# A mixer layer on one core: conditioning weights in 2 MB pieces summed partly on TensorE, and block 0's stores issued from ScalarE's queue

## The chip, the cores and the metric

The kernel runs on one core of a Trainium2 chip. It uses TensorE (PE) for matrix products, VectorE (DVE), ScalarE (ACT) and GpSimd (POOL) for the element work, and SyncE (SP) mostly for issuing DMA transfers. The metric is device time in microseconds (us) of one execution; the median of 3 runs is what counts. Lower is better.

## The reference, cut to what matters

One layer (DEPTH is 1) on a sequence of 2048 tokens with 1024 features, in float32. The conditioning vector `c` gives shift, scale and gate (adaLN); the normalised input goes through one combined input projection into three groups of heads; their outputs are gated, concatenated, projected and added back:

```
mod = silu(c) @ w_ada + b_ada        # 1024 x 3072: shift, scale, gate
h   = rmsnorm(x, norm_g) * (1 + scale) + shift
u   = h @ w_in + b_in                # columns: mLSTM v,q,k,o,z; i,f gates; FoX; conv
A: mLSTM, 4 heads x 128 (q and k after a 4-tap convolution), chunk by chunk
B: forgetting attention, 4 heads x 64
C: 256 channels: a * sigmoid(g), 31-tap causal depthwise convolution, norm, silu
x   = x + gate * (concat(A, B, C) * silu(z) @ w_out);   out = rmsnorm(x, final_g)
```

## The kernel before, in words

The tokens are cut into 4 blocks of 512 (`TB`), the 1024 features into 8 tiles of 128 (`KT`). A product of float32 numbers is made from three products of float32r parts: every operand is split into a high part (a cast on ACT) and a low part (a subtraction), and hi·hi, hi·lo and lo·hi are summed on PE.

**The start of block 0.** `hprep(0, ada_k)` loads the four x tiles, normalises them, and then makes for each feature tile k the transposed input `hh0_k` (high) and `hl0_k` (low): four PE transposes `xT`, an ACT activation `hf = xT*gs + shift` (L148), an ACT cast `hh` (L151), a subtraction `hl` (L152). The two columns `gs` and `shift` of tile k come from `ada_k(k)`: the 1024 x 128 pieces of `w_ada` for shift and scale are loaded (tile `wa`, L747, two transfers of 512 KB for each k), multiplied by silu(c) and summed over 8 row groups: two of them start the sums on ACT (`wacc`, L772), six are added on DVE (L775), the two sums are added (L777), transposed on PE (`pt_ada`, L780), reduced on DVE (L782) and finished by three column operations (L784, L785, L787).

**The units of a block.** The input projection is cut into units of 256 columns or so. Their order is fixed: v (with the mLSTM gate columns), ca and cg (convolution group, value and gate), mv, mo, two qk units, mz, then mv to mz again for the other two heads, and the FoX and conv-gate units. A unit is 48 PE products of 512 columns, or 96 of 256. In block 0, `split_unit` gets the weights: for each half it loads 0.5 MB of raw weights into `wr` (L174, two buffers), casts the high part on ACT (L181) and subtracts the low part on POOL (L182), giving a 1 MB tile `w2`, three of which exist; it then stores that tile to DRAM as `wd` (L183), and blocks 1 to 3 load it from there instead of splitting again. Weights of a unit are fetched one unit or more ahead by `prefetch()`.

**After the v unit**, `gates()` runs scans on DVE (L350, L356, L363) and exponentials on ACT, and stores three small tables (`nb`, `rr`, `ir`, L352, L373, L374). **The convolution** of a block follows cg: for each of two channel tiles 31 taps; in block 0, 6 of these are products on ACT (`tp`, L458) added up on POOL (`ap`, L459), and the other taps are DVE operations (`ac`, L461, 24 and a first one on ACT). The qk units have a convolution of 4 taps on DVE (`am`, L552 and L556). The tiles `am` are transposed on PE (`pk`, L591) and multiplied with each other (`psT`, L595) in the mLSTM steps.

**What sets the order.** The program is written in stages, and the framework's scheduler decides in which order each engine gets its instructions; each engine then runs its own list in order. So an instruction that waits holds up everything behind it on its engine. On PE, `psT` and `pk` of the first two heads stand between the last product of the first mz unit and the first product of the second mv unit (`mv0_1`); this is so before and after the change. Before the change, all transfers that matter here are issued from SP: loads of raw weights, stores of split weights, and the loads of x for block 1 (`x1`, L129), whose normalisation (L135 to L138) is done as soon as the tiles have landed.

Of the kernel before, what the change touches and what calls it, by code (L numbers as in the profile page):

```python
# [16 lines left out]
P = 128  # L17
# [21 lines left out]
def tile_hybrid_trunk(  # L39
# [21 lines left out]
    v, s, g, pe, dma = nc.vector, nc.scalar, nc.gpsimd, nc.tensor, nc.sync  # L61
# [49 lines left out]
    wraw = left1.enter_context(tc.tile_pool(name="wraw", bufs=WRB))  # L111
# [11 lines left out]
    def hprep(b, pre=None):  # L123
# [34 lines left out]
    w_d = {}  # L158
# [5 lines left out]
    def split_unit(name, pieces, pool):  # L164
# [5 lines left out]
        for hf in range(2):  # L170
            wr = pool.tile([P, 4, 268], F32, name=f"wr_{name}_{hf}", tag="wr", bufs=WRA if pool is not wraw else 2)
            o = 0
            for col, n in pieces:
                dma.dma_start(  # L174
                    wr[:, :, o : o + n],
                    dram(w_in, hf * 4 * P * DIN + col, [[DIN, P], [P * DIN, 4], [1, n]]),
                )
                o += n
            flat, w4 = unit_tile(name, hf, width)
            wh, wl = w4[:, 0], w4[:, 1]  # L180
            s.copy(wh, wr[:, :, 0:width])  # L181
            (v if name in WLV else g).tensor_tensor(wl, wr[:, :, 0:width], wh.bitcast(F32), op=ALU.subtract)  # L182
            dma.dma_start(w_d[key][hf], flat.bitcast(F32))  # L183
            whs.append(wh)
            wls.append(wl)
# [127 lines left out]
    def unit_v(b, h):  # L313
        w = load_unit(f"v{b}")
        for tt in range(NTT):
# [13 lines left out]
            dma.dma_start(v_d[b * NTT + tt], vs.bitcast(F32))  # L329

    def gates(b, G):
# [20 lines left out]
        dma.dma_start(nb_d[:, b * TB : (b + 1) * TB], nbr)  # L352
# [20 lines left out]
        dma.dma_start(rr_d[b], rr)  # L373
        dma.dma_start(ir_d[b], ir)  # L374
# [284 lines left out]
    def wout_steps():  # L659
# [3 lines left out]
        def flat(name):  # L663
            return wraw.tile([P, 4, 268], F32, name=name, tag="wr", bufs=2).rearrange("p a e -> p (a e)")[:, 0:D]
# [49 lines left out]
    with tc.tile_pool(name="ada", bufs=4, side="right") as apool:  # L714
# [44 lines left out]
        def ada_k(j):  # L759
            if j < 0:  # L760
                for i in range(PRE):
                    ada_load(i)
                return
            if j == 0:
                for i in range(PRE, WAB):
                    ada_load(i)
            elif j + WAB - 1 < KT:
                ada_load(j + WAB - 1)
            wt = wts[j]
            accs = [apool.tile([P, 2, P], F32, name=f"wacc{j}{e}", tag=f"wacc{e}", bufs=2) for e in range(2)]  # L770
            for k in range(2):
                s.activation(accs[k], wt[:, k], AF.Identity, scale=csil[:, k : k + 1])  # L772
            for k in range(2, KT):
                a = accs[k % 2]
                v.scalar_tensor_tensor(a, wt[:, k], csil[:, k : k + 1], a, op0=ALU.mult, op1=ALU.add)  # L775
            acc = accs[0]
            v.tensor_tensor(acc, acc, accs[1], op=ALU.add)  # L777
# [415 lines left out]
WRB = 2  # L1193
# [45 lines left out]
```

## Time and profile before

| | us |
|---|---|
| median of 3 runs | 1372.14 (1370.55 to 1374.48) |
| the profiled execution | 1372.62 |
| its span in the profile | 1370.8 |
| PE busy | 1278.7 (93%) |
| DVE busy | 961.0 (70%) |
| ACT busy | 570.3 (42%) |
| POOL busy | 345.1 (25%) |
| mean DMA rate over the span | 220 GB/s |

The profile was taken of one execution, 0.5 us over the median; 1.8 us of its time lie outside its span. The page cuts the span in 40 slices of 34.3 us. PE is busy in 3, 7, 4 and 7 tenths of the first four slices, and in 9 or more in nearly all others. Stretches of time are given in us from the start of the span. In the rows that follow a line such as `L461` is the line of the kernel before, and `a<-b,c` says that tile a is written from tiles b and c.

### The profile page before, as it was taken

To read this page: it belongs to the slowest core of one execution; us is meant where nothing else is said; L and a number is where in the kernel's file an instruction comes from. 1 tells how busy PE (TensorE), PEld (TensorE's weight loads), DVE (VectorE), ACT (ScalarE), POOL (GpSimd) and SP (SyncE) were. 2 spreads that over 40 slices of the span, in tenths; PEclk is the share of its full clock that TensorE was granted. 3 is DMA by queue.
4 is the path that set the end of the run, shared out by engine and by line. 5 is a ranking of instruction groups with operands and counts; after the bars stand their busy time and mean duration, and the time that the engine had idled before them with its cause. 6 is when DMAs were issued, how large, how long until landed. Compare 5 with 4: busy or idle time off the path is not lost. (4 is left out here: it accounts for less than half of the span.)

```text
span 1370.8 us, 21119 instructions
## 1 busy us (share of the span) xinstructions
PE 1278.7 (93%) x7383; PEld 1112.9 (81%) x7383; DVE 961.0 (70%) x2473; ACT 570.3 (42%) x1204; POOL 345.1 (25%) x398
## 2 busy tenths in 40 slices
PE   3747999999999999999999999998989999999997
PEld 2637898887889888989888889988868888878886
DVE  6789948748997655794662796674786677866742
ACT  4472434354233236330314232224575565655631
POOL 3466545510132010050110070121131211211121
PEclk9977999999999999999999999999999999999999
DMA  9947768699897469564558764469986454644141
GB/s 266 321 170 235 239 231 292 230 320 397 305 347 246 155 221 314 186 214 167 188 189 270 217 242 173 168 228 326 294 263 183 152 173 143 198 149 134 62 131 62
DMA packets 151874, 301.62 MB, mean 220 GB/s; under 512 B 14968, under 2 KB 92072, under 8 KB 133592
## 3 DMA queue, kind: packets, MB, share of 16 engines
q1 hardware_dynamic: 151768, 300.28, 65.4%
q8 instruction: 58, 0.95, 0.3%
q14 instruction: 48, 0.39, 0.1%
HBM read 224.54 MB, written 75.69 MB: 219 GB/s over the span
## 5 line engine op out<-in xcount | busy, mean ns | idle before, releaser
L461 DVE SCALAR_TENSOR_TENSOR ac<-ca,dww,ac 128x512 f32<-128x512 f32 x228 | 181.5, 831 | 2.4 <-ACT ac L446 1.9
L1063 PE MATMUL po<-wo,yh 128*128 128x512 f32 x512 | 164.7, 397 | 1.0 <-ACT yh L1053 0.7
L287 PE MATMUL pc_qk<-hh,w_qk 128*128 128x512 f32 x512 | 163.1, 395 | 0.3 <-DMA w_qk<-wd_qk 0.3
L299 PE MATMUL pt_mv<-w_mv,hh 128*128 128x256 f32 (+1 forms) x512 | 100.4, 297 | 29.2 <-ACT w_mv L181 10.5
L879 ACT ACTIVATE S<-S,mx 128x512 f32<-128x512 f32 (+3 forms) x160 | 103.7, 651 | 52.4 <-DVE mx L877 48.8
L287 PEld LDWEIGHTS pc_qk<-hh,w_qk 128*128 128x128 f32 x512 | 96.2, 188 | 21.0 <-DMA w_qk<-wd_qk 0.6
L1063 PEld LDWEIGHTS po<-wo,yh 128*128 128x128 f32 x512 | 94.1, 188 | 21.0 <-ACT yh L1053 0.9
L299 PEld LDWEIGHTS pt_mv<-w_mv,hh 128*128 128x128 f32 x512 | 84.7, 202 | 31.1 <-ACT w_mv L181 10.9
L927 DVE TENSOR_TENSOR tl<-ptr,th 128x512 fp32r<-128x512 f32 (+1 forms) x144 | 92.4, 654 | 24.7 <-ACT th L926 23.7
L1063 PE MATMUL po<-wo,ya 128*128 128x512 f32 x256 | 101.1, 396 | 0.0
L299 PE MATMUL pt_mo<-w_mo,hh 128*128 128x256 f32 x512 | 96.9, 290 | 4.3 <-DMA w_mo<-wd_mo 2.2
L287 PE MATMUL pc_qk<-hl,w_qk 128*128 128x512 f32 x256 | 100.8, 394 | 0.0
L926 ACT CAST th<-ptr 128x512 fp32r<-128x512 f32 (+1 forms) x144 | 76.3, 561 | 51.2 <-PE ptr L918 50.3
L552 DVE SCALAR_TENSOR_TENSOR am<-um,cols,am 128x512 f32<-128x512 f32 x96 | 83.4, 877 | 10.1 <-ACT am L549 9.3
L918 PE MATMUL ptr<-ident,S 128*128 128x128 f32 x544 | 84.1, 275 | 4.8 <-DVE tl L927 3.4
L299 PEld LDWEIGHTS pt_mo<-w_mo,hh 128*128 128x128 f32 x512 | 82.0, 196 | 4.8 <-DMA w_mo<-wd_mo 2.4
L287 PE MATMUL pc_f<-hh,w_f 128*128 128x512 f32 x256 | 84.8, 400 | 0.0
L869 POOL TENSOR_SCALAR_AFFINE_SELECT nd<-n 128x128 f32<-128x128 f32 (+1 forms) x64 | 30.5, 479 | 208.4 <-DVE mx L872 129.0
L287 PE MATMUL pc_mz<-hh,w_mz 128*128 128x512 f32 x256 | 82.7, 395 | 0.0
L299 PE MATMUL pt_mv<-w_mv,hl 128*128 128x256 f32 (+1 forms) x256 | 74.7, 293 | 0.0
L299 PE MATMUL pt_mo<-w_mo,hl 128*128 128x256 f32 x256 | 73.4, 289 | 0.0
L918 PEld LDWEIGHTS ptr<-ident,S 128*128 128x128 f32 x544 | 64.5, 142 | 10.1 <-DVE tl L927 2.8
(267 smaller groups left out, 3245.0 us busy)
## 6 DMA issues: line engine op xcount, KB each, us to landing
w_qk<-wd_qk SPq DMA_DIRECT2D x24, 1024.0 KB
w_mo<-wd_mo SPq DMA_DIRECT2D x12, 1024.0 KB
w_mz<-wd_mz SPq DMA_DIRECT2D x12, 1024.0 KB
w_f<-wd_f SPq DMA_DIRECT2D x12, 1024.0 KB
w_mv<-wd_mv SPq DMA_DIRECT2D x10, 1024.0 KB
n<-nb_d SPq DMA_DIRECT2D x36, 256.0 KB
wa<-in_w_ada_dram SPq DMA_DIRECT2D x16, 512.0 KB
x<-in_x_dram SPq DMA_DIRECT2D x16, 512.0 KB
```

Of the source, the lines that this page charges most:

```text
L287: pe.matmul(ps, a, r, start=(n == 0), stop=(n == 3 * KT - 1))
L299: pe.matmul(ps[:, 0:width], a[:, cs], r, start=(n == 0), stop=(n == 3 * KT - 1))
L461: backlog.append(lambda acc=acc, u=u, i=2 * j + m, j=j: v.scalar_tensor_tensor(acc, u[:, j : j + TB], dww[:, i : i + 1], acc, op0=ALU.mult ...
L552: v.scalar_tensor_tensor(acc, u[:, j : j + TB], cols[:, r + 8 * j : r + 8 * j + 1], acc, op0=ALU.mult, op1=ALU.add)
L869: g.affine_select(out=nb[:, 0:Wq], in_=L["n", ch][:, 0:Wq], pattern=[[-1, Wq]], compare_op=ALU.is_ge, fill=NEG, base=t0 - ch * TB, channel ...
L879: s.activation(Sb[:, 0:Wq], Sb[:, 0:Wq], AF.Exp, bias=mx[:, 4:5], accum_out=mx[:, 8 + ch : 9 + ch])
L918: pe.transpose(pt[:, i, qi * P : (qi + 1) * P], Ps[qi][0][kk // TB][:, kk % TB : kk % TB + P], ident)
L926: s.copy(f(th), f(pt))
L927: v.tensor_tensor(f(tl), f(pt), f(th.bitcast(F32)), op=ALU.subtract)
L1063: pe.matmul(po, a, w[:, ns], start=(i == 0), stop=(i == 3 * KT - 1))
```

## The change

**The conditioning weights.** `w_ada` is loaded in four pieces of 2 MB instead of eight of 1 MB: one piece holds 256 columns of shift and 256 of scale, so the contiguous run in DRAM is 1 KB and not 512 bytes. A piece serves two feature tiles at once. Of its 8 row groups, one starts the sum on ACT (128x512), four are added by DVE operations of 128x512, and the last three are summed by PE, in products whose moving operand is one column of silu(c); a product of the DVE sum with a column of ones adds the rest. These are 16 products for a piece, straight in the layout of `shift` and `gs`, so the transpose and the reduction are gone. Three DVE operations on two columns finish the pair.

**The queues in block 0.** `sdma` is ACT's queue. From it are issued the stores of split weights, of v (L329) and of the three gate tables, the rows of small constants, the 8 and 4 column pieces of the v unit, and three of the later loads. The other loads stay on SP, so that the raw weight loads of block 0 follow one another there. The loads of `x1` are put behind the raw weights of `mz0_1` in the order of issue.

**The order of prefetches.** `ca0` gets its raw tiles from another pool and is fetched between the third and the fourth piece of `w_ada`; v between the first and the second.

```diff
-    v, s, g, pe, dma = nc.vector, nc.scalar, nc.gpsimd, nc.tensor, nc.sync
+    v, s, g, pe, dma, sdma = nc.vector, nc.scalar, nc.gpsimd, nc.tensor, nc.sync, nc.scalar
...
-            dma.dma_start(xt, x[0, b * TB + tt * P : b * TB + (tt + 1) * P, :])
+            with tc.issue_after(wload["mz0_1"]) if b == 1 else ExitStack():
+                dma.dma_start(xt, x[0, b * TB + tt * P : b * TB + (tt + 1) * P, :])
...
-                dma.dma_start(
-                    wr[:, :, o : o + n],
+                ins = (dma if n > 8 else sdma).dma_start(
+                    raw[:, :, o : o + n],
...
+                if n > 8:
+                    wload[name] = ins.ins
...
-            s.copy(wh, wr[:, :, 0:width])
-            (v if name in WLV else g).tensor_tensor(wl, wr[:, :, 0:width], wh.bitcast(F32), op=ALU.subtract)
-            dma.dma_start(w_d[key][hf], flat.bitcast(F32))
+            s.copy(wh, raw)
+            g.tensor_tensor(wl, raw, wh.bitcast(F32), op=ALU.subtract)
+            sdma.dma_start(w_d[key][hf], flat.bitcast(F32))
...
-            dma.dma_start(v_d[b * NTT + tt], vs.bitcast(F32))
+            (dma if b else sdma).dma_start(v_d[b * NTT + tt], vs.bitcast(F32))
...
-        dma.dma_start(nb_d[:, b * TB : (b + 1) * TB], nbr)
+        gdma = dma if b else sdma
+        gdma.dma_start(nb_d[:, b * TB : (b + 1) * TB], nbr)
...
-        dma.dma_start(rr_d[b], rr)
-        dma.dma_start(ir_d[b], ir)
+        gdma.dma_start(rr_d[b], rr)
+        gdma.dma_start(ir_d[b], ir)
...
-        def ada_load(j):
-            wt = apool.tile([P, KT, 2, P], F32, name=f"wa{j}", tag="wa", bufs=WAB)
+        def ada_load(jp):
+            wt = apool.tile([P, KT, 2, 256], F32, name=f"wa{jp}", tag="wa", bufs=WAB)
             for i in range(2):
-                dma.dma_start(wt[:, :, i, :], dram(w_ada, i * D + j * P, [[3 * D, P], [P * 3 * D, KT], [1, P]]))
+                dma.dma_start(wt[:, :, i, :], dram(w_ada, i * D + jp * 256, [[3 * D, P], [P * 3 * D, KT], [1, 256]]))
             wts.append(wt)
...
+        def ada_k(j):
+            if j < 0:
+                ada_load(0)
+                return
+            if j == 0:
+                prefetch(apool)
                 for _ in range(3):
-                    dma.dma_start(*later.pop(0))
-            if j == CAJ:
+                    sdma.dma_start(*later.pop(0))
+                ada_load(1)
+                ada_load(2)
                 prefetch(apool)
-            if j == KT - 1:
+                ada_load(3)
                 for a in later:
                     dma.dma_start(*a)
...
-            accs = [apool.tile([P, 2, P], F32, name=f"wacc{j}{e}", tag=f"wacc{e}", bufs=2) for e in range(2)]
-            for k in range(2):
-                s.activation(accs[k], wt[:, k], AF.Identity, scale=csil[:, k : k + 1])
-            for k in range(2, KT):
-                a = accs[k % 2]
-                v.scalar_tensor_tensor(a, wt[:, k], csil[:, k : k + 1], a, op0=ALU.mult, op1=ALU.add)
-            acc = accs[0]
-            v.tensor_tensor(acc, acc, accs[1], op=ALU.add)
+            jp = j // 2
+            wt = wts[jp]
+            acc = apool.tile([P, 2, 256], F32, name=f"wacc{j}", tag="wacc", bufs=2)
+            s.activation(acc, wt[:, 0], AF.Identity, scale=csil[:, 0:1])
+            for k in range(1, NKD):
+                v.scalar_tensor_tensor(acc, wt[:, k], csil[:, k : k + 1], acc, op0=ALU.mult, op1=ALU.add)
             pta = psx.tile([P, 512], F32, name=f"pt_ada{j}", tag="x")
             for i in range(2):
-                pe.transpose(pta[:, i * P : (i + 1) * P], acc[:, i, :], ident)
-            red = apool.tile([P, 2], F32, name=f"red{j}", tag="red", bufs=3)
-            v.reduce_sum(red, pta[:, 0:256].rearrange("p (a e) -> p a e", e=P), axis=AX.X)
+                for a in range(2):
+                    o = 2 * i + a
+                    cs = slice(a * P, (a + 1) * P)
+                    for k in range(NKD, KT):
+                        pe.matmul(pta[:, o : o + 1], wt[:, k, i, cs], csil[:, k : k + 1], start=(k == NKD), stop=False)
+                    pe.matmul(pta[:, o : o + 1], acc[:, i, cs], one, start=False, stop=True)
...
-            v.tensor_tensor(shift[:, j : j + 1], red[:, 0:1], cols[:, r : r + 1], op=ALU.add)
...
+            v.tensor_tensor(shift[:, j : j + 2], pta[:, 0:2], cols[:, r : r + 2], op=ALU.add)
...
+NKD = 5
+WAB = 4
```

The program that results has 63 instructions fewer on DVE (2210), 54 fewer on SP (550), 38 more on ACT (906) and 24 more on PE (5986). Three places show how the scheduler has placed them. In these rows a name such as `w2_ca0_0` is a tile (here the split weights of the first half of unit ca0; numbers behind it are the program's own), and the arrow points from what is read to what is written.

The first is ACT at the end of block 0's start, where the last four tiles of its input are made. Before:

```order
L148 ACTIVATE hf0_4_403<-xT0_4_398,shift_83,gs_82 128x512
L181 CAST w2_ca0_0_266<-wr_ca0_0_264 128x1024
L772 ACTIVATE wacc70_469<-wa7_260,csil_84 128x256
L151 CAST hh0_4_405<-hf0_4_403 128x512
L148 ACTIVATE hf0_5_433<-xT0_5_428,shift_83,gs_82 128x512
L151 CAST hh0_5_435<-hf0_5_433 128x512
L181 CAST w2_ca0_1_272<-wr_ca0_1_270 128x1024
L148 ACTIVATE hf0_6_463<-xT0_6_458,shift_83,gs_82 128x512
```

and after:

```order
L773 ACTIVATE wacc6_391<-wa3_231,csil_84 128x512
L184 CAST w2_ca0_0_220<-wr_ca0_0_219 128x1024
L149 ACTIVATE hf0_4_374<-xT0_4_369,shift_83,gs_82 128x512
L152 CAST hh0_4_376<-hf0_4_374 128x512
L186 DMA wd_ca0_218<-w2_ca0_0_220 128x2048
L149 ACTIVATE hf0_5_385<-xT0_5_380,shift_83,gs_82 128x512
L152 CAST hh0_5_387<-hf0_5_385 128x512
L149 ACTIVATE hf0_6_422<-xT0_6_417,shift_83,gs_82 128x512
```

The store of ca0's first half (L186) now stands on ACT ahead of `hf0_5`; it can be issued once POOL has subtracted the low part of that half. On SP the raw tiles of cg0 are loaded ahead of those of ca0.

The second is POOL where the convolution begins. Before:

```order
L444 COPY halo_c_86<-ca0_0_754 128x30
L459 TENSOR_TENSOR ap0_0_828<-ap0_0_828,tp0_0_1_830 128x512
L459 TENSOR_TENSOR ap0_0_828<-ap0_0_828,tp0_0_2_833 128x512
L459 TENSOR_TENSOR ap0_0_828<-ap0_0_828,tp0_0_3_836 128x512
L444 COPY halo_c_86<-ca0_1_781 128x30
L459 TENSOR_TENSOR ap0_0_828<-ap0_0_828,tp0_0_4_839 128x512
L182 TENSOR_TENSOR w2_mv0_0_0_786<-wr_mv0_0_0_784,w2_mv0_0_0_786 128x1024
L459 TENSOR_TENSOR ap0_0_828<-ap0_0_828,tp0_0_5_842 128x512
L583 AFFINE_SELECT E0_0_1436<-E0_0_1436 128x512
L182 TENSOR_TENSOR w2_mv0_0_1_792<-wr_mv0_0_1_790,w2_mv0_0_1_792 128x1024
```

and after:

```order
L185 TENSOR_TENSOR w2_cg0_1_664<-wr_cg0_1_663,w2_cg0_1_664 128x1024
L185 TENSOR_TENSOR w2_mv0_0_0_725<-wr_mv0_0_0_724,w2_mv0_0_0_725 128x1024
L448 COPY halo_c_86<-ca0_0_694 128x30
L185 TENSOR_TENSOR w2_mv0_0_1_731<-wr_mv0_0_1_730,w2_mv0_0_1_731 128x1024
L463 TENSOR_TENSOR ap0_0_768<-ap0_0_768,tp0_0_1_770 128x512
L587 AFFINE_SELECT E0_0_1376<-E0_0_1376 128x512
L463 TENSOR_TENSOR ap0_0_768<-ap0_0_768,tp0_0_2_773 128x512
L185 TENSOR_TENSOR w2_mo0_0_0_836<-wr_mo0_0_0_835,w2_mo0_0_0_836 128x1024
```

The subtractions for both halves of mv now come ahead of the chain of convolution taps (`ap`) instead of behind four and five of its links; mo's first half comes behind the second link.

The third is DVE between the end of the v unit and the convolution. Before:

```order
L339 TENSOR_TENSOR G0_510<-G0_510,ab0_660 128x4x2x4
L135 TENSOR_TENSOR ss1_0_2515<-s21_0_2510 128x1
L136 TENSOR_SCALAR ss1_0_2515<-ss1_0_2515 128x1
L138 TENSOR_SCALAR x1_0_2508<-x1_0_2508,ss1_0_2515 128x1024
L135 TENSOR_TENSOR ss1_1_2527<-s21_1_2522 128x1
L136 TENSOR_SCALAR ss1_1_2527<-ss1_1_2527 128x1
L135 TENSOR_TENSOR ss1_2_2539<-s21_2_2534 128x1
L136 TENSOR_SCALAR ss1_2_2539<-ss1_2_2539 128x1
L138 TENSOR_SCALAR x1_1_2520<-x1_1_2520,ss1_1_2527 128x1024
L350 SCALAR_TENSOR_TENSOR grwk0_672<-one_74,ncar_88,pg0_667 4x512
```

and after:

```order
L342 TENSOR_TENSOR G0_450<-G0_450,ab0_600 128x4x2x4
L353 SCALAR_TENSOR_TENSOR grwk0_612<-one_74,ncar_88,pg0_607 4x512
L360 SCALAR_TENSOR_TENSOR grE0_613<-one_74,pg0_607 4x128 x4
L354 COPY ncar_88<-grwk0_612 4x1
L362 TENSOR_TENSOR T2_452<-pg0_607,grE0_613 4x512
L367 SCALAR_TENSOR_TENSOR grhv0_614<-one_74,mp0_616,T2_452 4x128
L368 TENSOR_TENSOR mp0_616<-grE0_613,grhv0_614 4x1
```

The normalisation of block 1's x is gone from here (it stands after the qk units now), and the scans of the gates follow at once, in one piece ahead of the convolution.

More of the change, by code (lines that the diff above doesn't have):

```diff
@@ L110, in tile_hybrid_trunk @@
     left1 = ExitStack()
-    wraw = left1.enter_context(tc.tile_pool(name="wraw", bufs=WRB))
+    wraw = left1.enter_context(tc.tile_pool(name="wraw", bufs=2))
     hpool = left1.enter_context(tc.tile_pool(name="hpool", bufs=1))
@@ L155, in hprep @@
         return hi, lo
-    w_d = {}
+    w_d, wload = {}, {}
     def unit_tile(name, hf, width):
@@ L170, in split_unit @@
         for hf in range(2):
-            wr = pool.tile([P, 4, 268], F32, name=f"wr_{name}_{hf}", tag="wr", bufs=WRA if pool is not wraw else 2)
+            raw = pool.tile([P, 4, 268], F32, name=f"wr_{name}_{hf}", tag="wr", bufs=2)[:, :, 0:width]
+            flat, w4 = unit_tile(name, hf, width)
+            wh, wl = w4[:, 0], w4[:, 1]
             o = 0
             for col, n in pieces:
-                dma.dma_start(
-                    wr[:, :, o : o + n],
+                ins = (dma if n > 8 else sdma).dma_start(
+                    raw[:, :, o : o + n],
                     dram(w_in, hf * 4 * P * DIN + col, [[DIN, P], [P * DIN, 4], [1, n]]),
                 )
+                if n > 8:
+                    wload[name] = ins.ins
                 o += n
[L179 to L183, printed above, removed]
+            s.copy(wh, raw)
+            g.tensor_tensor(wl, raw, wh.bitcast(F32), op=ALU.subtract)
+            sdma.dma_start(w_d[key][hf], flat.bitcast(F32))
             whs.append(wh)
@@ L238, in tile_hybrid_trunk, with prefetch @@
     side = []
-    def prefetch(pool=wraw):
+    def prefetch(pool=None):
         if upos[0] < len(useq):
@@ L663, in flat @@
         def flat(name):
-            return wraw.tile([P, 4, 268], F32, name=name, tag="wr", bufs=2).rearrange("p a e -> p (a e)")[:, 0:D]
+            return wraw.tile([P, 4, 268], F32, name=name, tag="wr").rearrange("p a e -> p (a e)")[:, 0:D]
         def ada_load(k):
@@ L727, in tile_hybrid_trunk @@
             if r < R_BQK:
-                dma.dma_start(r1[r : r + n, :], rows(ap, off, n))
+                sdma.dma_start(r1[r : r + n, :], rows(ap, off, n))
             else:
@@ L756, in ada_load @@
                 for a in later:
                     dma.dma_start(*a)
[L759 to L762, printed above, removed]
+            if j % 2:
                 return
[L764 to L769, printed above, removed]
-            accs = [apool.tile([P, 2, P], F32, name=f"wacc{j}{e}", tag=f"wacc{e}", bufs=2) for e in range(2)]
-            for k in range(2):
-                s.activation(accs[k], wt[:, k], AF.Identity, scale=csil[:, k : k + 1])
-            for k in range(2, KT):
-                a = accs[k % 2]
-                v.scalar_tensor_tensor(a, wt[:, k], csil[:, k : k + 1], a, op0=ALU.mult, op1=ALU.add)
-            acc = accs[0]
-            v.tensor_tensor(acc, acc, accs[1], op=ALU.add)
+            jp = j // 2
@@ L783, in ada_k @@
             r = R_BADA + j
-            v.tensor_tensor(shift[:, j : j + 1], red[:, 0:1], cols[:, r : r + 1], op=ALU.add)
-            v.scalar_tensor_tensor(gs[:, j : j + 1], red[:, 1:2], cols[:, r + 8 : r + 9], one,
-                                   op0=ALU.add, op1=ALU.add)
-            v.tensor_tensor(gs[:, j : j + 1], gs[:, j : j + 1], cols[:, R_NG + j : R_NG + j + 1], op=ALU.mult)
+            v.tensor_tensor(shift[:, j : j + 2], pta[:, 0:2], cols[:, r : r + 2], op=ALU.add)
+            v.tensor_tensor(gs[:, j : j + 2], pta[:, 2:4], cols[:, r + 8 : r + 10], op=ALU.add)
@@ L789, in tile_hybrid_trunk @@
+            v.scalar_tensor_tensor(gs[:, j : j + 2], gs[:, j : j + 2], 1.0, cols[:, R_NG + j : R_NG + j + 2],
+                                   op0=ALU.add, op1=ALU.mult)
         h = hprep(0, ada_k)
@@ L1198 @@
 SZB = 3
-WLV = ()
 ORD = 1
```

10 lines of the change are left out of this document (1 added, 9 removed).

## The prediction

> **What bounds the kernel now.** I first cut the span into stretches. Columns: the stretch and its length, busy us (and instructions) of PE, PE weight load, DVE, ACT and POOL, the granted clock of PE, the DMA share, GB/s.
>
> ```profile
> 0.00:20.00 20.00, 2.89 (x7) 1.20 (x7) 10.19 (x32) 10.51 (x25) 3.92 (x17) 1.00 0.93 268
> 20.00:40.00 20.00, 11.65 (x45) 9.59 (x46) 16.82 (x37) 7.76 (x14) 8.03 (x5) 1.00 1.12 270
> 40.00:60.00 20.00, 15.23 (x76) 13.01 (x75) 15.68 (x33) 8.97 (x14) 9.47 (x6) 0.91 0.91 289
> 60.00:68.00 8.00, 8.00 (x57) 7.38 (x56) 3.15 (x11) 2.45 (x3) 4.59 (x14) 1.00 1.03 420
> 68.00:175.00 107.00, 79.11 (x417) 69.27 (x416) 98.40 (x133) 50.04 (x94) 65.11 (x42) 0.86 0.65 220
> 83.00:120.00 37.00, 12.09 (x76) 11.59 (x76) 35.56 (x42) 16.36 (x29) 33.02 (x17) 0.70 0.47 159
> 175.00:1370.00 1195.00, 1161.80 (x6790) 1012.51 (x6788) 816.77 (x2231) 490.53 (x1056) 253.99 (x317) 0.99 0.64 216
> ```
>
> From 175 us on PE is busy for 1161.8 of 1195 us: it is the bound there, and the change leaves its work alone. Before that PE idles for about 30 us up to 60 and 28 us between 68 and 175. Any gain must come from there.
>
> In 68 to 175 the busy engine is DVE, 98.4 of 107 us. Its largest groups there (busy us, mean ns of one):
>
> ```profile
> L461 DVE SCALAR_TENSOR_TENSOR ac<-ca,dww,ac 128x512 f32<-128x512 f32 x48 | 51.5, 1111 | 0.1
> L552 DVE SCALAR_TENSOR_TENSOR am<-um,cols,am 128x512 f32<-128x512 f32 x12 | 15.4, 1299 | 2.9 <-ACT am L549 2.7
> L138 DVE TENSOR_SCALAR x<-x,ss 128x1024 f32<-128x1024 f32 x4 | 3.0, 744 | 0.7 <-POOL ss L137 0.7
> ```
>
> These operations are not as long everywhere. Over the whole program the same two lines have medians of 743 and 746 ns (after the counts: shortest, median, longest):
>
> ```profile
> L461 DVE SCALAR_TENSOR_TENSOR ac<-ca,dww,ac x228: 712/743/2954, 84.8 to 830.7; 128x512 f32<-128x512 f32 x114
> L552 DVE SCALAR_TENSOR_TENSOR am<-um,cols,am x96: 715/746/2911, 152.7 to 870.5; 128x512 f32<-128x512 f32 x96
> ```
>
> So 48 x (1.111 - 0.743) = 17.7 us and 12 x (1.299 - 0.746) = 6.6 us of DVE's time are stretching. POOL is busy meanwhile:
>
> ```profile
> L459 POOL TENSOR_TENSOR ap<-ap,tp 128x512 f32<-128x512 f32 x10 | 17.8, 1778 | 4.7 <-ACT tp L458 4.4
> L182 POOL TENSOR_TENSOR w_qk<-wr_qk,w_qk 128x1024 fp32r<-128x1024 f32 x4 | 10.7, 2680 | 14.3 <-ACT w_qk L181 14.3
> L182 POOL TENSOR_TENSOR w_mv<-wr_mv,w_mv 128x1024 fp32r<-128x1024 f32 x3 | 7.3, 2434 | 0.4 <-ACT w_mv L181 0.4
> ```
>
> In the timeline seven taps take 13.5 us instead of 5.2, while POOL runs taps and splits:
>
> ```profile
> 105.13 13.49 DVE L461 SCALAR_TENSOR_TENSOR ac<-ca,dww,ac 128x512 f32<-128x512 f32 x7
> ```
>
> DVE is what PE meets at the end of the stretch, in the mLSTM transposes:
>
> ```profile
> 173.60 0.69 DVE L556 SCALAR_TENSOR_TENSOR am<-tm,am 128x512 f32<-128x512 f32 x1 [0.70 <-ACT tm L555]
> ...
> 174.02 0.40 PE L287 MATMUL pc_mz<-hh,w_mz 128*128 128x512 f32 x1
> 174.25 0.60 PE L591 MATMUL pk<-ident,am 128*128 128x128 f32 x4
> ...
> 175.58 0.60 PE L591 MATMUL pk<-ident,am 128*128 128x128 f32 x4
> ```
>
> PE is at these transposes at 174.25 and needs the last `am` (ready at 174.3) at 175.58: the two arrive together. PE's named waits in 60 to 175 us are four (us in total, times, longest):
>
> ```profile
> PE pt_mv L299 <- ACT w_mv L181: 10.5, 1, 10.5
> PE pt_mv L299 <- POOL w_mv L182: 8.5, 1, 8.5
> PE pt_mv L299 <- DVE v L514: 6.8, 1, 6.8
> PE pt_mo L299 <- DVE v L514: 2.1, 1, 2.1
> ```
>
> They are 27.9 us, all of PE's idle time there. But PE, freed of them, meets DVE's `am` in front of `mv0_1` and waits there instead. So **I take the gain as what DVE's last `am` of that step comes earlier**; the rest of the program moves with it.
>
> **The start of block 0.** Two times mark it:
>
> ```profile
> 62.32 0.62 ACT L151 CAST hh<-hf 128x512 fp32r<-128x512 f32 x1
> ...
> 67.94 0.17 DVE L306 TENSOR_TENSOR G<-pt_v,btok 128x12 f32<-128x12 f32 x1 [2.75 <-PE pt_v L299]
> ```
>
> The last input tile is ready at 62.9; the v unit's products end at 67.9. Removed from DVE are most of these, seen between 7 and 62 us:
>
> ```profile
> L775 DVE SCALAR_TENSOR_TENSOR wacc<-wa,csil,wacc 128x256 f32<-128x256 f32 x48 | 22.2, 512 | 6.4 <-ACT wacc L772 6.4
> L777 DVE TENSOR_TENSOR wacc<-wacc,wacc 128x256 f32<-128x256 f32 x8 | 6.3, 782 | 0.0
> L784 DVE TENSOR_TENSOR shift<-red,cols 128x1 f32<-128x1 f32 x8 | 4.3, 537 | 0.1
> L782 DVE TENSOR_REDUCE red<-pt_ada 128x2 f32<-128x256 f32 x8 | 3.3, 417 | 2.9 <-PE pt_ada L780 2.9
> L785 DVE SCALAR_TENSOR_TENSOR gs<-red,cols,one 128x1 f32<-128x1 f32 x8 | 2.8, 347 | 0.0
> L787 DVE TENSOR_TENSOR gs<-gs,cols 128x1 f32<-128x1 f32 x8 | 2.3, 289 | 0.1
> ```
>
> Together 41.2 us. Added are 16 operations of 128x512 and 12 on two columns: 16 x 0.743 + 12 x 0.3 = 15.5 us, or 21 with the stretched 1.11. ACT's 16 activations of 128x256 become 4 of twice the width. On PE 64 products with one moving column replace 16 transposes. No row has that shape; the nearest are transposes in plain float32, whose 32 products here leave two records each:
>
> ```profile
> L942 PE MATMUL pb<-ident,rt x64: 270/275/422, 976.2 to 1308.7; 128*128 128x128 f32 x64
> ```
>
> Two records of 0.275 are 0.55 us for 128 columns if nothing overlaps, and one column can take less: an upper bound of 16 x 0.55 = 8.8 us a piece, a lower one of 16 x 0.27 = 4.3 (one record, the second behind it). I take 5. Only the last group's delay counts; the others run while the next piece arrives.
>
> When does the last piece land? Ahead of `ca0` the queue carries 8.4 MB of `w_ada`, 2.1 of x and 1.1 of v, 11.6 MB as before. At 270 GB/s that is 43 us, at 347 (midway from there to the 420 of 60 to 68 us) 33; I take 38. Then the chain for the last two tiles: ACT start (1.0), four DVE operations (3 to 4.4), PE's group (5), three small ones (1), transposes and, on ACT, `hf`, `hh`: 4 tiles x 1.4 = 5.6. ACT's order has the cast of ca0 and the store of its first half ahead of `hf5`; that store waits for a POOL split of 2.4, and the cast for raw tiles queued behind cg0's, at about 44. So ACT gets to `hf4` at 45 and, with the store's hold, to the end of `hh7` at 45 + 5.6 + 2.4 = 53 if nothing slips and at 56 if it does. With bounds of 48 (no hold) and 63 (as now) I take the v unit's end at 58, after a value of 54.5 for the last tile and 3.5 for the products behind it: **gain 67.9 - 58 = 9.9**.
>
> The Trainium skill ("DMA: Bandwidth & Descriptors", "Specifications") puts the smallest transfer for line rate at 512 bytes; by it the 1 KB runs bring nothing. The last piece would land 4.5 us later, at 42.5, and the time below would be about 1363. The rows lean the other way: 270 GB/s at a share of 1.12 in 20 to 40 us, with the 512-byte runs in flight, and 420 at 1.03 behind them, when 4 KB rows of x and 8 KB rows of split weights ran.
>
> **From the v unit to the last `am`.** Before, this takes 174.3 - 67.9 = 106.4 us. The scans began at 78.8, behind normalisations of x1:
>
> ```profile
> 78.82 1.27 DVE L350 TENSOR_TENSOR_SCAN grwk<-one,ncar,pg 4x512 f32<-4x512 f32 x1
> ```
>
> That is 10.9 us after the v unit. Now ca's 40 remaining products (0.23 each, the step from 174.02 to 174.25 above; 9.1) stand between, plus the gate transposes: 10. Gain 1. The x1 work leaves the stretch: 3.0 us of L138 and 1.2 of small ones; but while DVE waits for cg's gate some 3 of it was cover, and I book 1.7 in all. The splits of mv (two of 2.4) run ahead of the convolution, when DVE waits for cg, so they no longer stretch its taps: of 4.8, 60%, the share in which DVE and POOL hinder one another (28 us lost, counting 4 on small groups, in 47 us of taps and splits): 2.9. Against this, PE, which reaches the transposes some 10 us early and waits there, comes out with a low clock, as in 83 to 120 us (0.70, PE busy 12.1 of 37): 5 us at half pace, 2.3. Net 1 + 1.7 + 2.9 - 2.3 = **3.3**.
>
> Stores leave SP: 16 issues. SP's rows show what they cost there:
>
> ```profile
> 102.93 0.32 SPq L183 DMA_DIRECT2D wd_mv<-w_mv  x1
> 103.30 0.43 SPq L174 DMA_DIRECT2D wr_mo<-in_w_in_dram  x1
> ```
>
> The load behind a store goes out 0.4 us after it, and its raw buffer comes free with the very POOL split that the store waits for. I book nothing for it; the cover is DVE, which is late anyway, and without that cover it is 16 x 0.37 = 5.9. The Trainium skill says the same in "DMA: Bandwidth & Descriptors", "Issuing engines are not separate DMA queues": another issuing engine saves only issue time on the first. By it the whole gain is that of the start, 1372.6 - 9.9 = 1362.7.
>
> On ACT each store waits, with ACT's later work behind it (taps `tp`, evacuations, the next cast), for POOL's subtraction, which was cast just before it. I count 9 such stores between the convolution's start and the transposes, 2.5 us each, or 4.3 where POOL has a tap of 1.78 in front. Bounds: 0 (ACT is busy only 50 of 107 us) and 9 x 4.3 = 39. DVE does 48 taps meanwhile that need no ACT result, so I take 0.
>
> The x1 work, 4.2 us of DVE, moves to behind 175 us, where DVE is busy 817 of 1195; cover enough, 4.2 without it.
>
> Sum: 9.9 + 3.3 = 13.2. From the profiled execution's 1372.6, half a us over the median of 1372.1: **1359**, its span 1357.8. Own range: 5 us less of the start (mark at 63) gives 1364, 3 more for the stretch 1367; 5 more of the start and the 4 us that small groups are stretched give 1350.
>
> **Rivals.**
>
> *DVE is freed more than I book.* If the reordered splits leave POOL's taps and DVE's less in each other's way, PE's 27.9 us of idle time come back less a few, on top of the start's 9.9: 1335 at the extreme, 1345 with half to two thirds. For it: 24 us of stretching in two lines. Against: POOL's work is the same in amount, and has to run somewhere in the same 100 us.
>
> *The change doesn't do what it says.* ACT's store hold and ca0's late arrival put the last tile at 62 again, and the queues bring nothing: 1372.6 less 2 to 3, 1370. For it: the chain above has 7 us of slack at most between 56 and 63, and before the change the rows of tile 7 were held by PE's own ca products, not DVE. Against: DVE is freed of 20 us.
>
> *Slower: ACT is held behind stores.* The place is ACT between the convolution's start and `pk`. Each of 9 stores holds ACT until POOL is through; `tp` is late, so POOL's tap chain is late, so its next split too. On the path 9 x 4.3 = 39 us; with half of that, 19.5 - 13.2 = 6.3 slower, 1379. It decides once more than 3 of the 9 holds lie on the path (3 x 4.3 = 13). For it: POOL already sat 14.3 us waiting for ACT's casts of qk. Against: ACT is idle for 57 us of 107.
>
> **How the numbers follow.** My forecast has 0.50, the first rival 0.25, the second 0.14, the third 0.11. A change of under 0.3% (4 us) can't be told from none here. Forecast and first rival are faster by more than that, except 0.03 of the forecast's upper tail; of the second rival 0.05 is faster (1368 or less), of the third 0.02 no change. Faster 0.50 - 0.03 + 0.25 + 0.05 = 0.77, same 0.03 + 0.09 + 0.02 = 0.14, slower 0.09. The range reaches from 1342, under the first rival's 1345, to 1372, over the second's.
>
> **What would show it.** Last cast `hh` at 53 to 56; `G` from v at about 58; DVE work on `w_ada` of 15 to 21 us; the first scan 10 us behind the v unit. L465 (the taps) with a mean of about 1.05 us. The two waits for `w_mv` (19 us) gone, and a new one of about 10 us at `pk` or `psT` for DVE's `am`; the transposes of that step near 162. ACT's idle time ahead of `tp` and of casts: if POOL is named there for over 13 us, the third rival holds. I am wrong if PE doesn't wait at `pk` (DVE isn't the pace), if PE's idle time behind 175 us grows, or if the last `hh` comes at 62 again.

## The result: 0.9% slower, and the start of block 0 is where it was lost

The changed kernel takes 1384.52 us (median of 4 runs, 1381.18 to 1390.11) against 1372.19: the ratio is 1.0093, with a 95% interval of 1.0064 to 1.0122. The profiled execution took 1386.11, its span 1384.3. A gain of 13 us was forecast; the loss is 12.

The stretches of the changed kernel, cut where the marks of the prediction fall (columns as there):

```profile
20.00:40.00 20.00, 7.78 (x34) 7.04 (x34) 8.79 (x15) 4.73 (x11) 8.26 (x5) 1.00 0.93 295
40.00:60.00 20.00, 18.90 (x99) 18.45 (x100) 12.94 (x14) 7.14 (x12) 8.76 (x5) 0.78 0.64 231
60.00:80.00 20.00, 20.00 (x117) 19.50 (x116) 3.50 (x14) 6.64 (x9) 4.09 (x3) 0.71 0.13 54
...
81.40:182.00 100.60, 81.19 (x417) 70.13 (x416) 92.87 (x117) 45.24 (x77) 65.66 (x49) 0.90 0.63 220
```

In 20 to 40 us PE, DVE and ACT are all less busy than before (PE 7.8 of 20 against 11.7, DVE 8.8 against 16.8, ACT 4.7 against 7.8): everybody waits for something. In 60 to 80 PE is busy throughout, but at a granted clock of 0.71, and the transfers have all but stopped (54 GB/s). The kernel before had there:

```profile
60.00:80.00 20.00, 20.00 (x112) 17.23 (x111) 12.46 (x39) 13.91 (x34) 9.73 (x20) 1.00 0.87 347
```

The marks in the timeline of the changed kernel:

```profile
75.73 0.62 ACT L152 CAST hh<-hf 128x512 fp32r<-128x512 f32 x1
...
81.40 0.17 DVE L309 TENSOR_TENSOR G<-pt_v,btok 128x12 f32<-128x12 f32 x1 [0.34 <-POOL G L806]
...
187.96 0.48 PE L302 MATMUL pt_mv<-w_mv,hh 128*128 128x256 f32 x2
```

The last of them is PE's first product behind the mLSTM transposes, which before was this row:

```profile
175.94 0.48 PE L299 MATMUL pt_mv<-w_mv,hh 128*128 128x256 f32 x2
```

The last input tile of block 0 is ready at 76.4 instead of 62.9, the v unit ends at 81.4 instead of 67.9 (13.5 later), and the first product behind the transposes comes 12.0 later. From there the delay changes by less than 2 us: the first transposes `pb`, at 976.2 before, are 13.9 later in this execution,

```profile
L943 PE MATMUL pb<-ident,rt x64: 270/275/421, 990.1 to 1322.0; 128*128 128x128 f32 x64
```

and the span is 13.5 longer. So the loss comes from the first 81 us. From the v unit to the first product behind the transposes the changed kernel is even 1.4 us quicker.

**What ACT does there.** The timeline of ACT in the changed kernel (start, length, idle time before and what ended it; ACTq are transfers that ACT issues):

```profile
2.04 4.36 ACTq L177 DMA_DIRECT2D wr_v<-in_w_in_dram  x2
6.44 0.54 ACTq L761 DMA_DIRECT2D bfv<-in_b_in_dram  x1
7.02 3.27 ACTq L177 DMA_DIRECT2D wr_v<-in_w_in_dram  x2
13.61 1.53 ACTq L761 DMA_DIRECT2D btok<-in_b_in_dram  x2
15.17 1.28 ACT L742 ACT_TABLE_LOAD   x1 [15.17 <-DMA wr_v<-in_w_in_dram]
16.46 0.21 ACT L742 ACTIVATE ct<-cols 128x8 f32<-128x8 f32 x1
...
22.09 2.06 ACT L184 CAST w_v<-wr_v 128x1072 fp32r<-128x1072 f32 x2
38.48 0.83 ACTq L186 DMA_DIRECT2D wd_v<-w_v  x2
39.41 1.45 ACT L149 ACTIVATE hf<-xT,shift,gs 128x512 f32<-128x512 f32 x2 [15.27 <-DMA r<-in_c_ln_g_dram]
```

Two holds stand out. Silu(c), the first thing that the conditioning needs (`ct`), comes at 16.5 us, since now ACT issues ten small transfers first; before it came at 3.7:

```profile
3.72 0.21 ACT L738 ACTIVATE ct<-cols 128x8 f32<-128x8 f32 x1 [1.71 <-DVE cols L736]
```

And ACT does nothing from 24.2 to 38.5: the two stores of v's split weights stand in front of the first `hf`. POOL had finished the split long before, and what the profile names as the releaser is a transfer of SP, a row of constants that has nothing to do with v:

```profile
24.60 5.31 POOL L185 TENSOR_TENSOR w_v<-wr_v,w_v 128x1072 fp32r<-128x1072 f32 x2
...
37.61 0.25 SPq L767 DMA_DIRECT2D r<-in_c_ln_g_dram  x1
```

In the program's list of instructions, with what each waits for, the link is plain. Every transfer, of whichever queue, is given one of eight completion counters in turn, and one that gets a counter again waits until the transfer that had it has landed (a row that waits for DMAHW7 also takes that counter over). ACT's rows, and SP's last ones that had the same two counters:

```
ACT  L186 DMA wd_v0_192<-w2_v0_0_194 128x2144 [waits DMAHW7_49,Pool_49]
ACT  L186 DMA wd_v0_192<-w2_v0_1_202 128x2144 [waits DMAHW1_49,Pool_49]
ACT  L149 ACTIVATE hf0_0_278<-xT0_0_273,shift_83,gs_82 128x512 [waits DVE_49,PE_49]
SP   L767 DMA r3_129<-in_m_conv_w_dram 32x128 [waits DMAHW7_49]
SP   L767 DMA r3_129<-in_c_ln_g_dram 2x128 [waits DMAHW1_49]
```

Both of SP's rows are issued behind all of `w_ada`, at 36.9 and 37.6 us. On SP alone, as before the change, such a wait only holds SP. On ACT's queue it holds ACT's computing. By the same list, six of the ten small transfers ahead of silu(c) wait for a counter too.

### The profile page after: what moved, and what is told of

It reads as the page before. It is cut to its first block, busy times and chain, and to the rows that moved or that the text cites. A ratio compares the mean times of both kernels' runs of the same rounds, so it can differ in the third digit from the quotient of the medians.

```text
span 1384.3 us, 21228 instructions
## 1 busy us (share of the span) xinstructions
PE 1299.1 (94%) x7495; PEld 1135.1 (82%) x7495; DVE 941.6 (68%) x2413; ACT 566.3 (41%) x1192; POOL 339.9 (25%) x398
## 5 line engine op out<-in xcount | busy, mean ns | idle before, releaser
L465 DVE SCALAR_TENSOR_TENSOR ac<-ca,dww,ac 128x512 f32<-128x512 f32 x228 | 185.3, 850 | 3.3 <-ACT ac L450 2.9
L556 DVE SCALAR_TENSOR_TENSOR am<-um,cols,am 128x512 f32<-128x512 f32 x96 | 78.6, 827 | 8.5 <-ACT am L553 8.0
```

What stands on the lines that cost most here:

```text
L465: backlog.append(lambda acc=acc, u=u, i=2 * j + m, j=j: v.scalar_tensor_tensor(acc, u[:, j : j + TB], dww[:, i : i + 1], acc, op0=ALU.mult ...
L556: v.scalar_tensor_tensor(acc, u[:, j : j + TB], cols[:, r + 8 * j : r + 8 * j + 1], acc, op0=ALU.mult, op1=ALU.add)
```

## The experiments

Theory A: the loss is ACT's hold in front of the stores of v's weights. Theory B: it is the late silu(c). Theory C: it is PE's 16 products with one moving column for each piece of `w_ada`. Ratios are against the kernel before, with their 95% intervals.

| edit of the changed kernel | us | ratio | last `hh` done | v unit's end |
|---|---|---|---|---|
| none | 1384.5 | 1.0093 (1.0064 to 1.0122) | 76.4 | 81.4 |
| small loads on SP | 1391.6 | 1.0124 (1.0081 to 1.0167) | 79.1 | 84.5 |
| v's stores on SP | 1374.5 | 1.0022 (1.0003 to 1.0040) | 65.9 | 71.0 |
| both | 1371.4 | 0.9997 (0.9975 to 1.0019) | 63.6 | 69.0 |
| all on SP | 1373.7 | 1.0012 (0.9986 to 1.0037) | 65.1 | 70.4 |
| other counters for v's stores | 1375.5 | 1.0032 (1.0010 to 1.0053) | 66.7 | 71.8 |
| v's stores on ACT, behind `hh` | 1375.1 | 1.0043 (1.0021 to 1.0066) | 64.9 | 72.8 |
| all on SP, 8 groups on DVE | 1366.4 | 0.9958 (0.9937 to 0.9980) | 59.7 | 65.1 |
| the same, ca0's loads first | 1366.1 | 0.9970 (0.9954 to 0.9986) | 57.8 | 62.3 |

The last two columns are read from one execution of each edit, whose own time is up to 5 us off the median in the second column.

### One hold taken away, then the other, then both

```diff
-                sdma.dma_start(r1[r : r + n, :], rows(ap, off, n))
+                dma.dma_start(r1[r : r + n, :], rows(ap, off, n))
-                ins = (dma if n > 8 else sdma).dma_start(
+                ins = dma.dma_start(
-                    sdma.dma_start(*later.pop(0))
+                    dma.dma_start(*later.pop(0))
```

> The changed kernel, but the rows of constants, the narrow pieces of the v unit and the three later loads are issued from SP again; every store stays on ACT. Theory A (the loss is ACT's hold in front of the store of v's split weights, 24 to 38.5 us, until a transfer of SP that uses the same completion counter has landed): the second v store still holds ACT until such a transfer lands, so the last hh comes 0 to 4 us earlier than 76.4, 1381 to 1385. Theory B (the loss is silu(c), done at 16.9 us because ACT issues ten small transfers first): silu(c) at about 5 us and everything 8 to 10 us earlier, 1374 to 1376. Theory C (PE's 16 products with one moving column cost 4 to 8 us a piece): no change, 1384.

1391.6 us. Silu(c) is early (`ct` at 3.8 us), and nothing is gained: ACT then stands at the first store until 40.7.

```profile
3.77 0.21 ACT L742 ACTIVATE ct<-cols 128x8 f32<-128x8 f32 x1 [1.75 <-DVE cols L740]
...
40.72 0.34 ACTq L186 DMA_DIRECT2D wd_v<-w_v  x1
41.11 0.62 ACT L152 CAST hh<-hf 128x512 fp32r<-128x512 f32 x1 [15.79 <-DMA r<-in_m_conv_w_dram]
```

The releaser is again one of SP's rows of constants, the one that had the first store's counter. Theory B falls as the main cause. The run is even slower than any theory allowed: the hold ends 2.2 us later than in the changed kernel, since SP now issues the small loads too, and the v unit ends 3.1 later. At the mLSTM transposes PE then waits 3.7 us for DVE's `am`, which it didn't in the changed kernel, and the span is 4.7 longer; the medians are 7 apart, and what makes up the difference isn't in the trace.

```diff
-            sdma.dma_start(w_d[key][hf], flat.bitcast(F32))
+            (dma if name in ('v0',) else sdma).dma_start(w_d[key][hf], flat.bitcast(F32))
```

> The changed kernel, but the two stores of the v unit's split weights are issued from SP. Theory A: ACT isn't held at 24 us, the first hf comes at about 29 instead of 39.4 us, the last hh 8 to 11 us earlier, 1374 to 1376. Theory B: silu(c) is still late at 16.9 us, so no more than 2 us are gained, 1382 to 1384. Theory C: 1384.

1374.5 us, as theory A had it: the first `hf` comes at 29.9 instead of 39.4, and the v unit ends 10.4 us earlier.

```profile
29.91 0.78 ACT L149 ACTIVATE hf<-xT,shift,gs 128x512 f32<-128x512 f32 x1 [5.92 <-DVE gs L787]
```

Both edits together:

> Both edits together: the small loads and the two v stores on SP, the other stores of block 0 on ACT. Theories A and B together: the last hh at 53 to 60 us, as the prediction had it, 1359 to 1368. Theory C: the products of one column keep it at 66 or later, 1374 or more.

1371.4 us, no difference from the kernel before. Behind the removed store, the early silu(c) is now worth something: the v unit ends another 2.0 us earlier in the trace. A and B together are the whole loss. But the last `hh` comes at 63.6, not at 53 to 60: the new sum of the conditioning weights brings nothing in this place, and theory C is still alive.

```diff
-    v, s, g, pe, dma, sdma = nc.vector, nc.scalar, nc.gpsimd, nc.tensor, nc.sync, nc.scalar
+    v, s, g, pe, dma, sdma = nc.vector, nc.scalar, nc.gpsimd, nc.tensor, nc.sync, nc.sync
```

> The changed kernel with every transfer on SP: only the new sum of the conditioning weights, the order of prefetches and the late x1 loads are left of the change. The start as with both edits (A and B: last hh at 53 to 60). If the stores on ACT behind the v unit are worth something, this is 1 to 5 us slower than with both edits; if they hold ACT up, as much faster. 1359 to 1370 by A and B, 1374 or more by C.

1373.7 us, not to be told from the run before it.

### What the store waits for

The edit leaves everything on ACT's queue. Only the order of SP's loads changes: ca0's raw weights go ahead of the rows of constants and of cg0's. By the program's list the two stores then have the counters of the first two transfers of the second piece of `w_ada`.

```diff
                 for a in later:
-                    dma.dma_start(*a)
+                    with tc.issue_after(wload["ca0"]):
+                        dma.dma_start(*a)
...
+                with tc.issue_after(wload["ca0"]) if name == "cg0" else ExitStack():
                     ins = (dma if n > 8 else sdma).dma_start(
```

> The changed kernel with all its stores and small loads on ACT as they were, and ACT's instructions up to 30 us in the same order: the two v stores still stand ahead of the first hf. Only SP's loads are put in another order (ca0's raw weights ahead of the twelve rows of constants, cg0's behind them), by which the two stores get the completion counters that the first two transfers of the second piece of w_ada used, landed by about 26 us, and not those of constants' rows that land at 38. If the store waits for the transfer that had its counter before (theory A's cause), it goes out when POOL has split v, at about 30 us, the first hf comes at 31 instead of 39.4, and the kernel takes 1373 to 1377. If the store waits for something else on ACT's queue (its own transfers, or a full queue), it is held to 36 to 39 us again, 1382 to 1386.

1375.5 us. The stores stand where they stood, ahead of the first `hf`, and go out as soon as POOL is through (at 30.1):

```profile
24.84 5.30 POOL L186 TENSOR_TENSOR w_v<-wr_v,w_v 128x1072 fp32r<-128x1072 f32 x2
...
27.31 3.19 ACTq L187 DMA_DIRECT2D wd_v<-w_v  x2
30.60 1.45 ACT L149 ACTIVATE hf<-xT,shift,gs 128x512 f32<-128x512 f32 x2 [6.22 <-DVE gs L789]
```

So it isn't ACT's queue as such, and not POOL: it is the transfer that had the counter before. In the changed kernel that happened to be one of SP's last loads of the start. The edit also brings ca0's weights earlier, which may have a part in the time, though not in when the stores go out; where only that was changed (the last row of the table), the median didn't move.

In the next edit `vlate` holds v's two stores, and `wload["hh"]` is the last cast of block 0's input; the lines that fill the two are left out:

```diff
...
+        for a in vlate:
+            with tc.issue_after(wload['hh']):
+                sdma.dma_start(*a)
```

> The small loads on SP; the two stores of v's split weights stay on ACT's queue, but behind the last cast hh of block 0 instead of ahead of it. Theory A (what costs is that the stores stand and wait ahead of hf and hh, not that ACT issues them): as with v's stores on SP, the last hh at 62 to 65 us, 1369 to 1374. If the queue itself is at fault: the last hh at 70 or later, 1380 or more.

1375.1 us (small loads on SP too). The last `hh` is done at 64.9, in the range of theory A: issued from ACT, but behind the urgent work, the stores don't hurt there. The time is a little over the range, and the trace names why: a tile of split weights is free only when its store has landed, so a late store holds the cast of ca0.

```profile
68.67 1.05 ACT L185 CAST w_ca<-wr_ca 128x1024 fp32r<-128x1024 f32 x1 [3.80 <-DMA wd_v<-w_v]
```

### PE's products with one column

```diff
-NKD = 5
+NKD = 8      # all row groups on ACT and DVE; the column of ones remains
```

> As the run with every transfer on SP, but all eight row groups of a piece are summed on ACT and DVE (seven DVE operations instead of four); PE keeps the 4 products with the column of ones for each piece, of 16. Theory C (the products of one column cost 4 to 7 us a piece and keep PE at half its clock): the last hh 5 to 8 us earlier than 65.1, at about 58, 1365 to 1369. Theory D (what holds the start is the arrival of the pieces and of ca0's raw weights): DVE's 3 more operations cost 2.2 us a piece, the last hh at 65 to 67, 1373 to 1376.

1366.4 us: 7.2 us less than with five groups, and 0.42% less than the kernel before. The groups of PE, first with five row groups on ACT and DVE, then with eight:

```profile
L782 PE MATMUL pt_ada<-csil,wa 128*128 128x1 f32 x96 | 20.7, 331 | 4.2 <-DMA wa<-in_w_ada_dram 3.8 <-ACT hf L149 0.4
...
L783 PE MATMUL pt_ada<-one,wacc 128*128 128x1 f32 x32 | 8.5, 335 | 5.5 <-DVE ss L137 5.5
```

```profile
L783 PE MATMUL pt_ada<-one,wacc 128*128 128x1 f32 x32 | 5.5, 294 | 16.2 <-DVE ss L137 14.2 <-DVE wacc L775 1.9
```

29.2 us of PE in place of 5.5, in the one stretch where v's products need PE; the three DVE operations more for each piece are hidden. Theory C holds for this part, and the v unit ends 5.2 us earlier. The rival there, that the pieces' arrival is the limit, had the last `hh` at 65 or later; it came at 59.7.

```diff
-pe.matmul(pta[:, o : o + 1], wt[:, k, i, cs], csil[:, k : k + 1], ...)
+pe.matmul(pta[:, o * 64 : o * 64 + 64], wt[:, k, i, cs], csil[:, k : k + 1].to_broadcast([P, 64]), ...)
```

> Every transfer on SP, five row groups on DVE as in the change, but each of the 16 products of a piece has 64 equal moving columns instead of one (the same sums, written 64 times). If a product's own length is what one column costs, 64 columns cost more and the last hh comes later than 65.1, 1374 to 1380. If one-column products leave PE idle enough for the granted clock to fall, the clock in 36 to 60 us rises from about 0.6 to 0.9 or more, and the products take no longer than with one column: 1366 to 1372.

1378.9 us (1.0070, 1.0044 to 1.0096), and no clear answer. The profiled execution, the quickest of its runs, has the v unit's end at 68.7, earlier than with one column (70.4), and its last group of 64-column products takes 3.7 us, where the last two groups of one column took 6.9 and 4.1 in the changed kernel; but the median is 5 us slower, and the clock in 36 to 60 us is 0.67, little above the 0.59 of the run with both edits. (The profile gives 0.90 for one column with every transfer on SP, but that can't be read: up to 51 us it says 1.00, while six one-column records take 1.44 us at 40.9 and half of that at 52.8.) What moves the median in the other executions isn't in the trace.

To the run with all eight groups on ACT and DVE:

```diff
+                with tc.issue_after(wload["ca0"]) if name == "cg0" else ExitStack():
                     ins = dma.dma_start(
...
```

> Every transfer on SP, all eight row groups summed on ACT and DVE (the fastest so far), and ca0's raw weights are issued ahead of the constants' rows and of cg0's. There ACT's cast of ca0 waited 4.0 us for its raw weights at 53 us in front of the last hh casts. If that wait is on the path, the last hh at 54 to 57 instead of 59.7 and 1361 to 1365; if PE's pace is, 1366.

1366.1 us (the constants' rows are behind ca0 too). The v unit ends another 2.9 us earlier, at 62.3, without a gain in the median. In the traces the lead is still there at the transposes `pb` (965.7 us against 968.8), and it is gone at the end (spans of 1360.7 and 1360.9). What takes it away in the last 395 us was not followed up.

### The queue, and x1, by themselves

```diff
+            (dma if name in ('v0', 'ca0') else sdma).dma_start(w_d[key][hf], flat.bitcast(F32))
```

> The small loads and the stores of v's and ca0's split weights on SP, the other stores of block 0 on ACT: nothing but compute on ACT before the v unit ends. If the hold at ca0's store (2 us in front of the last two hf) still counts, 1 to 2 us faster than with only v's stores on SP, 1369 to 1370; if not, the same 1371.

1373.3 us (1.0024, 1.0006 to 1.0043): ca0's stores on ACT cost nothing that can be told.

The same line in the kernel before, with its stores of v and the gate tables in block 0 on ACT:

> The kernel before, with only its stores behind the v unit (split weights from cg on, v, the three gate tables) issued from ACT: the queue part of the change without the start. By the prediction's booking (nothing for the queue) 1371 to 1373. If ACT held behind POOL's splits counts in the convolution, 1376 or more. If freeing SP counts, 1366 to 1370.

1373.8 us, 1.0026 (1.0010 to 1.0043): here stores issued from ACT behind the v unit cost 1.4 to 5.9 us. Freeing SP brought nothing.

The same line and `NKD = 8` in the changed kernel:

> All eight row groups on ACT and DVE, the small loads and the stores of v's and ca0's split weights on SP, and the other stores of block 0 on ACT: the queue part kept where ACT has nothing urgent. If stores behind the v unit cost nothing on ACT, 1366 as with every transfer on SP; if ACT held behind POOL's splits counts, 1369 or more; if freeing SP counts, 1362 to 1364.

1368.9 us, 0.9989 (0.9972 to 1.0006), 2.5 more than with every transfer on SP; the two intervals overlap a little. With five groups the sign was the other way (1371.4 with these stores on ACT, 1373.7 without), so the price of these stores is small and not settled.

```diff
-            with tc.issue_after(wload["mz0_1"]) if b == 1 else ExitStack():
+            with ExitStack():
```

> As the run with both edits (small loads and v's stores on SP), but the loads of block 1's x are not put behind the raw weights of mz0_1. By the prediction (1.7 to 4 us of DVE work back in the convolution's stretch) 1372 to 1375. If the late x1 work costs as much behind the stretch as it saves in it, 1371 again.

1372.3 us, 1.0006 (0.9987 to 1.0024), against 1371.4 with x1 late: no difference.

## Why the prediction was wrong

**The step that failed** is "ACT gets to `hf4` at 45" in the start of block 0. It counted what stands on ACT ahead of the last four tiles, and the quoted order began there. It did not look at what ACT issues earlier: ten small loads ahead of silu(c), and v's two stores ahead of the first `hf`. `hf4` came at 61.3:

```profile
61.34 0.78 ACT L149 ACTIVATE hf<-xT,shift,gs 128x512 f32<-128x512 f32 x1 [5.52 <-DVE gs L787]
```

With both groups on SP it comes at 46.5:

```profile
40.36 0.72 ACT L773 ACTIVATE wacc<-wa,csil 128x512 f32<-128x512 f32 x1 [0.25 <-DMA wa<-in_w_ada_dram]
46.50 0.78 ACT L149 ACTIVATE hf<-xT,shift,gs 128x512 f32<-128x512 f32 x1 [5.41 <-PE xT L147]
```

So the arrival of the pieces was priced nearly right (ACT starts on the last one at 40.4 there, 0.25 us after a wait for it; 38 was forecast), and the two holds cost 12.4 us of the v unit's end (81.4 against 69.0). The bounds of 48 and 63 had no term for it: a wait that the change adds had been put at POOL's split, 2.4 us, and never at a transfer of another queue.

**The rest of that sum was too small as well.** From `hf4` to the last `hh` the prediction had 8 to 11 us, and took 9.5; without the holds it took 17.1 (46.5 to 63.6). PE's group was put at 5 us a piece within 4.3 to 8.8; it measured 7.3 on average (29.2 for four), and "Only the last group's delay counts" was wrong: the third and fourth groups lie between v's products on PE, and both delay them. Taking the one-column products off PE gave 5.2 us back, and ca0's raw weights ahead of cg0's 2.9. From the 58 forecast for the v unit to the 70.4 with every transfer on SP are 12.4 us; these two account for 8.1, and the rest is open. DVE itself was freed as forecast (16.6 us of sums in place of most of 41.2), but the last tiles waited for PE: 5.4 us at `hf4` above. So even without the holds the kernel stood near the 1370 of the second rival (1371.4 and 1373.7), of whose reasons the late ca0 had a part.

**That the end of the program follows PE's first product behind the transposes** was right in the main. In the run with all eight groups on DVE that product comes at 166.94, 9.0 earlier than before; `pb` starts 7.4 earlier, and the profiled span is 9.9 shorter (this execution is 3.8 us quicker than the run's median).

```profile
166.94 0.49 PE L302 MATMUL pt_mv<-w_mv,hh 128*128 128x256 f32 x2
```

Set against the kernel before, the start of the next products (`pu`, at 188.3 before) and the span moved by the same amount within 1.7 us in eleven of the fourteen other traces, and within 3.7 us in all.

**That DVE's last `am` sets this product** failed, by the prediction's own sign: in the changed kernel PE doesn't wait at `pk`. The last `am` is ready at 185.2, and PE, which has waited 4.5 us at mz for POOL's split, comes to the transposes that need it only at 187.6:

```profile
184.47 0.69 DVE L560 SCALAR_TENSOR_TENSOR am<-tm,am 128x512 f32<-128x512 f32 x1
...
187.60 0.60 PE L595 MATMUL pk<-ident,am 128*128 128x128 f32 x4
```

In other runs it does wait there (4.8 us with eight groups on DVE and the late stores on ACT, 6.0 with x1 early).

**From the v unit to the transposes** a gain of 3.3 was booked; 1.4 was measured (108.0 to 106.6, to PE's first product behind the transposes). The scans came 9.3 us behind the v unit (10 forecast), and the two waits for `w_mv` are gone. But the wait of 6.8 us for DVE's `v` at mv is still there, the one at mo has grown from 2.1 to 6.9, and 4.5 us at mz for POOL's split are new. The wait of about 10 us at `pk` didn't come. PE's waits from the v unit to the transposes:

```profile
PE pt_mo L302 <- DVE v L518: 6.9, 2, 5.4
PE pt_mv L302 <- DVE v L518: 6.8, 1, 6.8
PE pc_mz L290 <- POOL w_mz L185: 4.5, 1, 4.5
PE pc_qk L290 <- POOL w_qk L185: 1.2, 1, 1.2
```

The term for the splits of mv ahead of the convolution fell: the taps are stretched more, not less, with a mean of 1.19 us (1.11 before, 1.05 forecast); the qk units' twelve are a little shorter (1.22 against 1.30).

```profile
L465 DVE SCALAR_TENSOR_TENSOR ac<-ca,dww,ac 128x512 f32<-128x512 f32 x48 | 54.8, 1189 | 1.1 <-ACT ac L450 1.0
L556 DVE SCALAR_TENSOR_TENSOR am<-um,cols,am 128x512 f32<-128x512 f32 x12 | 14.5, 1221 | 0.8 <-ACT am L553 0.7
```

**The queue was booked at nothing.** Alone, behind the v unit of the kernel before, it costs 1.4 to 5.9 us. The sentence from the Trainium skill ("DMA: Bandwidth & Descriptors", "Issuing engines are not separate DMA queues"), that another issuing engine saves only issue time, agrees as far as it goes: freeing SP gained nothing (1373.8 against 1371.1). It says nothing of what the issuing engine then waits for.

**The slower rival** named the mechanism, ACT held behind stores, but in the convolution and behind POOL. There it cost a few us at most, as the runs above show. It sat in the start, behind a transfer. Its 0.11 was too little: "ACT is busy only 50 of 107 us" is a mean, and a hold costs where ACT's next result is the one that everyone waits for. Whether the longer runs in DRAM helped can't be judged: no run has the old runs with the new sum. Two figures of the working are slips that change nothing: midway from 270 to 420 GB/s is 345, not 347, and 1370.8 less 13.2 is a span of 1357.6, not 1357.8.

## What to carry to other kernels

Before a transfer is moved to an engine that computes, list every transfer that the engine will issue with what it waits for, the completion counters shared with other queues too, and look at what computing stands behind each; a store put ahead of the first urgent result can wait for a load that has nothing to do with it. A sum moved to an engine that is idle on average has to be placed in that engine's order: here PE had idle time, but the products came between those that the end of the stretch waited for. And keep the parts of a change apart when measuring: the wider pieces, the new order of prefetches and the late x1, with the sum left on DVE and every transfer on SP, are together 0.4% quicker than the kernel before, which the whole change hid.

## What the runs showed of the hardware

Products of one column did not keep PE at its clock. In the changed kernel PE is busy without a gap through its last group (65.2 to 69.4 us), and the granted clock falls within it, 2.9 us after its first product; v's products behind it run at half pace for 5 us:

```profile
66.00:67.00 1.00, 1.00 (x11) 1.00 (x10) 0.00 (x0) 0.38 (x1) 0.54 (x1) 1.00 0.02 8
67.00:68.00 1.00, 1.00 (x11) 1.00 (x10) 0.00 (x0) 0.00 (x0) 0.73 (x1) 1.00 0.00 0
68.00:69.00 1.00, 1.00 (x7) 1.00 (x6) 0.00 (x0) 0.00 (x0) 0.00 (x0) 0.56 0.00 0
69.00:70.00 1.00, 1.00 (x7) 1.00 (x7) 0.39 (x3) 0.00 (x0) 0.00 (x0) 0.50 0.00 0
```

The traces with both groups of transfers on SP and with all on SP show the same fall, 3.0 and 2.3 us into that group. With 64 columns the group, 3.7 us long, ran to its end at full pace (its last six records with silu(c) are the second row). But two groups that began at half pace stayed there: one from 14.2 to 20.0 us, and one from 37.0 to 44.8, whose last six are the first row:

```profile
42.92 1.49 PE L782 MATMUL pt_ada<-csil,wa 128*128 128x64 f32 x6
...
51.56 0.83 PE L782 MATMUL pt_ada<-csil,wa 128*128 128x64 f32 x6
```

The Trainium skill ("TensorE: Matmul & The Clock Gate", Part 1) tells of a clock that is halved after about 3.4 us without work; these rows show it halved while the profile counts PE as busy. Whether the columns alone decide that was not settled.
